# Gate products of 20 more tiles made on chip in a decoder block with retrieved experts

## The chip, the core and the metric

The kernel runs on one core of one Trainium2 chip. The core has five engines with instruction streams of their own: TensorE (PE, matmuls), VectorE (DVE, elementwise work), ScalarE (ACT, activation functions and copies), GpSimd (POOL, here mostly gathers of table rows) and SyncE (SP, which issues transfers). They meet at semaphores. The metric is the time of one execution in device microseconds (us), median of several runs; lower is better.

## What is computed

One decoder block in fp32 over 512 tokens of 1024 channels. Three gated token mixers come first (forgetting attention, sliding-window attention, attention over a memory), and their merged output is added to the input. The change concerns what follows, a retrieval of experts:

```
def peer_ffn(h, w_q, keys1, keys2, u, v):
    q = (h @ w_q).reshape(B, S, PEER_HEADS, 2, half)
    ...
    sv, si = lax.top_k(cand, PEER_TOPK)
    experts = e1 * N_KEYS + e2
    gates = jax.nn.softmax(sv, axis=-1)
    ...
        a = jnp.einsum('cd,ced->ce', h_c, u[e_c])
        act = jax.nn.gelu(a, approximate=False) * g_c
        return jnp.einsum('ce,ced->cd', act, v[e_c])
```

Every token picks 8 x 16 = 128 of 16384 experts. For each of them it takes the dot product with a row of u, a gelu, the gate, and adds that multiple of a row of v.

## The kernel before

The 512 tokens are four blocks of 128. For blocks 0 and 1 the picked rows of u and v are gathered one by one by POOL (L833) and used by DVE: the dot product with a row of u is L843, the addition of a row of v is L852. A call of `step` uses one such row and has the next ones fetched, up to six ahead in the stage of the change (`AHEAD + MORE`), four ahead later.

Blocks 2 and 3 (256 tokens) are done densely over all experts, in 128 tiles of 128 experts. A tile k is one slice of u: eight matmuls of 128 x 128 by 256 tokens (`dense_u`, L971), then a gelu on ACT (L973) into `ga(k)`, a slot of 128 experts x 256 tokens. Slots 0 to 51 lie in the tile `soon`, later ones in `late`. In the end each slot is multiplied by the gates of its experts, zero for an expert that a token hasn't picked, and goes through the matmuls with v (`dense_v`).

The gates become dense in the spread stage, one loop over 64 groups of four tokens (run three ahead for the first part):

- `build_sides`: DVE compares a row of numbers with the picked expert's two indices, which gives two one-hot tiles `o` (L1026); ACT multiplies one by the gates (L1029).
- a call of `step` in four of five rounds (`STEPS_N` = 0.8).
- `spread`: PE multiplies the two one-hot tiles for each of the four tokens (L1041), which leaves in a bank of PSUM 128 gates of 128 tiles for each token. For the first `KEPT` = 32 tiles, whose activations are ready, DVE multiplies the gates straight into the slots (L1044, 32 tiles x 4 tokens). ACT copies the gates of the other 96 tiles to three stage tiles (L1047), and every eighth group SP writes these to memory (`gd`, L1051).
- four steps of the generator `dense_u`: one step to begin a tile, eight with a matmul each, one with the gelu. Ten steps make a tile, so 25 tiles (32 to 56) are computed beside 64 groups.

Behind it lies the v stage, a loop over the 128 tiles: for tile k the slot and the rows of v are split into high and low parts (L1089 and L1091 on ACT, L128 and L1094 on DVE), and PE makes 24 matmuls (L142 to L144). From tile 32 on, SP first reads the gates of four tiles at a time back (`gq`, L1065, two transfers each) and DVE multiplies (L1086). Tiles 57 to 127 of u run in this loop as well, every second one with split operands (L958, L960), and so do the remaining gathered rows.

PE, DVE and POOL run in the order in which the program is written from here on (`manual_schedule`); ACT and SP are ordered by the scheduler.

Of the kernel before, what the change touches and what calls it, by code (L numbers as in the profile page):

```python
# [7 lines left out]
F32 = mybir.dt.float32  # L8
# [4 lines left out]
AF = mybir.ActivationFunctionType  # L13
# [14 lines left out]
ND = len(DENSE)  # L28
TD = 128 * ND
FIRST_U, COVER, DURING, AFTER = 8, 24, 25, 0  # L30
KEPT = FIRST_U + COVER
SPILT = (128 - KEPT) // 3
AMONG, UNWEIGHED = 1.0, 14
LAG = FIRST_U + COVER + DURING + AFTER
GA_LATE = 6
# [10 lines left out]
GT = 4  # L46
TG = 32
GK = 4
WSLOT = 4 * 264
# [7 lines left out]
def tile_block(ctx: ExitStack, tc: tile.TileContext, t: dict, out: bass.AP):  # L57
    nc = tc.nc
    V, A, PE, G = nc.vector, nc.scalar, nc.tensor, nc.gpsimd
# [6 lines left out]
    wp = ctx.enter_context(tc.tile_pool(name="wp", bufs=3))  # L66
# [4 lines left out]
    def bank(tag):  # L71
        return psum.tile([128, 512], F32, tag=tag, name=tag, bufs=BANKS[tag])
# [26 lines left out]
    def load_raw(src, n):  # L99
        loads[0] += 1  # L100
        pool = early[0] if early and loads[0] % (RAW_MORE + 3) >= 3 else wp
        raw = pool.tile([128, WSLOT], F32, tag="raw", name="raw")
        fill(raw, src, n)
        return raw
# [35 lines left out]
    def mm3(ps, l, r, first=True, last=True):  # L140
        (lh, ll), (rh, rl) = l, r
        PE.matmul(ps, lh, rh, start=first, stop=False)  # L142
        PE.matmul(ps, lh, rl, start=False, stop=False)  # L143
        PE.matmul(ps, ll, rh, start=False, stop=last)  # L144
# [775 lines left out]
    soon = dp.tile([128, LAG + 1 - GA_LATE, TD], F32, name="ga", bufs=1)  # L920

    def ga(k):
        s = k % (LAG + 1)
        return soon[:, s] if s <= LAG - GA_LATE else late[0][:, s - (LAG + 1 - GA_LATE)]
# [11 lines left out]
        else:  # L936
            nc.sync.dma_start(u_raw[k], t["uT"][k])

    u_ring, u_next = [None, None], [FIRST_U]

    def fetch_u_to(k):
        while u_next[0] <= min(k, NK - 1):
            fetch_u(u_next[0])
            u_next[0] += 1

    def split_u(k):
        return k >= LAG and (k - LAG) % U_SPLIT > 0

    def dense_u(k):

        if k < FIRST_U:
            w = load_raw(t["uT"][k], D)[:, :D]
        else:
            fetch_u_to(min(k + URING - 1, LAG + 1) if k < LAG else k)
            w = u_raw.pop(k)
        if split_u(k):
            hi, lo = (gp[0].tile([128, D], F32R, tag=tag, name=tag, bufs=1) for tag in ("uhi", "ulo"))
            A.copy(hi, w)  # L958
            yield
            V.tensor_sub(lo, w, hi.bitcast(F32))  # L960
            yield
            ps, hi, lo = bank("mm"), *(x.rearrange("p (n w) -> p n w", n=KC) for x in (hi, lo))
            for dc in range(KC):
                mm3(ps[:, :TD], (hi[:, dc], lo[:, dc]), [x[dc] for x in h2s], dc == 0, dc == KC - 1)
            A.activation(ga(k), ps[:, :TD], AF.Gelu)
            return
        w = w.rearrange("p (n w) -> p n w", n=KC)
        yield
        ps = bank("mm")
        for dc in range(KC):  # L970
            PE.matmul(ps[:, :TD], w[:, dc], h2f[dc], start=dc == 0, stop=dc == KC - 1)  # L971
            yield
        A.activation(ga(k), ps[:, :TD], AF.Gelu)  # L973

    f = Found(found, BIG)
    h2T = [chunks(x) for x in pair(BIG)]
# [2 lines left out]
    with tc.tile_pool(name="qb", bufs=2) as qq:  # L979
        turn([x1[b] for b in GROUPS[1]], g2, *h2T)  # L980
        spent, dg, credit[0] = 0.0, None, 0.0
        for cost in search(qq, h2T, f, BIG):
            spent += cost
            if dg is None and spent > 12.0:
                V.tensor_copy(rstd[:, 1:NB], factors(sums, BIG))
                dg = diagonals(rstd[:, 2:NB], ND)
                turn([x1[b] for b in DENSE], g2, h2f, None, dg)
            credit[0] += cost
            while credit[0] >= PER_ROW and NJ <= done[0] < known[0]:
                credit[0] -= PER_ROW  # L990
                with tc.high_priority(-LATER):
                    step(apart=True)
            if k_u < FIRST_U and spent > 104.0 / FIRST_U * (k_u + 1):
                list(dense_u(k_u))
                k_u += 1
# [4 lines left out]
    gd = [dram.tile([128, NK // GK, 128 // TG, GK * TG], F32, name=f"gd{i}") for i in range(ND)]  # L1000


    slots, sides, stage = {}, {}, {}
# [4 lines left out]
    def turn_block(i):  # L1008

        ps = bank("acc")  # L1010
        b = DENSE[i]
        for k, src in enumerate((*chosen[b], gate[b])):
            PE.transpose(ps[:, k * 128:(k + 1) * 128], src, ident)
        eT = sp.tile([128, 3, 128], F32, tag="eT", name="eT", bufs=2)
        A.copy(eT.rearrange("p a b -> p (a b)"), ps[:, :384])
        slots[i] = eT

    def tokens(n):
        i, q = divmod(n, 128 // GT)
        return i, q * GT, slice(q * GT, (q + 1) * GT)  # L1020
# [11 lines left out]
    def spread(n):  # L1032
        i, t0, _ = tokens(n)
        o = sides.pop(n)
        if t0 % TG == 0:

            stage[0] = [wp.tile([128, WSLOT], F32, tag=tag, name="st")[:, :SPILT * TG].rearrange(
                "p (k t) -> p k t", t=TG) for tag in (("whi", "wlo") * 3)[n // (TG // GT) % 2 * 3:][:3]]
        ps = bank(("sc", "tp")[n % 2]).rearrange("p (t k) -> p t k", t=4)
        for u in range(GT):  # L1040
            PE.matmul(ps[:, u], o[:, 1, u], o[:, 0, u], start=True, stop=True)  # L1041
        c = t0 % TG
        kept = soon[:, :KEPT, i * 128 + t0:i * 128 + t0 + GT]
        V.tensor_mul(kept, ps[:, :, :KEPT].rearrange("p t k -> p k t"), kept)  # L1044
        for hf in range(3):
            k0 = KEPT + hf * SPILT
            A.copy(stage[0][hf][:, :, c:c + GT], ps[:, :, k0:k0 + SPILT].rearrange("p t k -> p k t"))  # L1047
        if c + GT == TG:
            for hf in range(3):
                k0 = KEPT + hf * SPILT  # L1050
                nc.sync.dma_start(gd[i][:, k0 // GK:(k0 + SPILT) // GK, t0 // TG],  # L1051
                                  stage[0][hf].rearrange("p (a k) t -> p a (k t)", k=GK))

    def get_gates(k, part):

        k -= k % GK
        if not KEPT <= k < NK or not 0 <= part < GQ_PARTS:
            return
# [52 lines left out]
    while k_u < FIRST_U + COVER:  # L1111
        if k_u == FIRST_U + UNWEIGHED:
            list(weigh(cp, f, 1))
        list(dense_u(k_u))
        k_u += 1
# [12 lines left out]
    spreading = ExitStack()  # L1128
    sp = spreading.enter_context(tc.tile_pool(name="sp", bufs=1))
    tile_u = None  # L1130
    turn_block(0)
    for n in range(AHD):
        build_sides(n)
    credit[0] = 0.0
    for n in range(AHD, NBAT + AHD):
        if n < NBAT:
            build_sides(n)
        if n == NBAT - PLAIN_ROWS:
            ahead[0] = AHEAD
        if n == NBAT - V_EARLY:  # L1140
            for k in range(VFAR):
                fetch_v(k)
        credit[0] += STEPS_N
        while credit[0] >= 1.0 and done[0] < known[0]:
            credit[0] -= 1.0
            step()
        if (n + 4) % PER == 0 and n + 4 < NBAT:
            turn_block((n + 4) // PER)
        spread(n - AHD)
        for _ in range(STEPS_U):  # L1150
            if tile_u is None and FIRST_U + COVER + n * DURING // NBAT >= k_u:
                tile_u = dense_u(k_u)
                next(tile_u)
                k_u += 1
            elif tile_u is not None and next(tile_u, 1):
                tile_u = None
    for _ in tile_u or ():
        pass
    share[0] = 0.0
    spreading.close()  # L1160
    gp = [ctx.enter_context(tc.tile_pool(name="gp", bufs=2))]
# [127 lines left out]
```

## Time and profile before

| | us |
|---|---|
| median of 3 runs (lowest, highest) | 1620.98 (1619.58, 1623.15) |
| profiled execution | 1613.45 |
| its span, first to last instruction | 1611.6 |
| spread stage, first one-hot tile to last gate product | 857.4 to 1004.1 |
| v stage, first matmul | 1006.5 |

The profile is of one execution; times in it are us from the span's start. The profiled execution is 7.5 us under the median of the runs. In a row of the timeline stand the start, the length, the engine, the line, the operation, the tile written and those read, and in brackets the idle time ahead of it with what ended it. A group's row has the busy time, the mean in ns and the idle time.

### The profile page before, as it was taken

The numbers are of one execution on the slowest core, as the hardware profiler recorded it, in microseconds if no ns is written. First come the engines' busy times: TensorE is split into PE (matmuls) and PEld (weight loads), VectorE is DVE, ScalarE is ACT, GpSimd is POOL, SyncE is SP. The second block draws the span as 40 slices with busy tenths as digits, with TensorE's granted clock in tenths as the row PEclk, the third lists the DMA queues.
The fourth block names the chain that finished last, engine by engine and source line by source line (L and its number), as shares of the span: only waits on it lengthen the run. The fifth ranks groups of instructions, "written<-read, shape, count | busy, mean of one in ns | idle before, by whom it ended". The sixth has DMA issues, their size and how long they took to land.

```text
span 1611.6 us, 26380 instructions
## 1 busy us (share of the span) xinstructions
PE 1532.9 (95%) x9030; PEld 1377.0 (85%) x9030; DVE 1406.2 (87%) x2721; ACT 782.9 (49%) x1782; POOL 780.6 (48%) x625
## 2 busy tenths in 40 slices
PE   5999999998998999998999999899999999999998
PEld 5999899988887989987888999688888888888887
DVE  5677458889888999999999999889899999999997
ACT  6787437645445443553116888344344343433432
POOL 1100011767566455588664333556655566555551
PEclk9999999999998999999999999999999999999999
DMA  8586753899998899967898999999999999999995
GB/s 300 176 283 223 236 196 118 285 358 310 326 344 287 280 360 342 326 203 264 320 404 304 367 385 350 379 394 394 399 409 407 395 411 408 410 412 409 406 407 215
DMA packets 180406, 531.85 MB, mean 330 GB/s; under 512 B 17456, under 2 KB 46384, under 8 KB 180272
## 3 DMA queue, kind: packets, MB, share of 16 engines
q0 software_dynamic: 73728, 268.47, 44.6%
q1 hardware_dynamic: 96752, 226.04, 38.6%
q10 hardware_dynamic: 9792, 35.66, 5.6%
q8 instruction: 71, 1.16, 0.3%
q14 instruction: 63, 0.52, 0.1%
HBM read 515.42 MB, written 14.68 MB: 329 GB/s over the span
## 4 chain that ended last, share of the span: by engine, by line
PE 36%; DVE 22%; DMA 17%; issue 15%; POOL 7%; ACT 2%; SPq 0%; DVEq 0%; POOLq 0%; ACTq 0%
DMA row<-in_peer_u_dram,eidx 8%; DMA row<-in_peer_v_dram,eidx 7%; POOL row L833 6%; PE mm L143 6%; PE mm L144 6%; PE mm L142 6%; DVE mg L852 6%; DVE o L1026 3%; DVE scr L843 3%; PE mm L971 3%; DVE wlo L128 2%; PE mm L295 2%; PE sc L142 1%; PE sc L143 1%; PE sc L144 1%
## 5 line engine op out<-in xcount | busy, mean ns | idle before, releaser
L833 POOL DMA_INDIRECT row<-in_peer_v_dram,eidx x256 | 346.0, 1351 | 269.2 <-DVE mg L852 150.0
L833 POOL DMA_INDIRECT row<-in_peer_u_dram,eidx x256 | 330.9, 1292 | 271.6 <-DVE scr L843 161.8
L843 DVE SCALAR_TENSOR_TENSOR scr<-row,own 128x1024 bf16<-128x1024 f32 x256 | 314.5, 1228 | 31.7 <-DMA row<-in_peer_u_dram,eidx 29.6
L128 DVE TENSOR_TENSOR wlo<-raw,whi 128x1024 fp32r<-128x1024 f32 (+1 forms) x243 | 305.6, 1259 | 36.3 <-ACT whi L116 35.7
L852 DVE SCALAR_TENSOR_TENSOR mg<-row,acts,mg 128x1024 f32<-128x1024 f32 x237 | 304.4, 1285 | 20.5 <-DMA row<-in_peer_v_dram,eidx 18.2
L971 PE MATMUL mm<-h2f,hhi 128*128 128x256 f32 x976 | 223.2, 379 | 1.6 <-ACT ga L973 1.6
L971 PEld LDWEIGHTS mm<-h2f,hhi 128*128 128x128 f32 x976 | 182.5, 190 | 26.6 <-ACT ga L973 2.0
L116 ACT CAST whi<-raw 128x1024 fp32r<-128x1024 f32 (+1 forms) x148 | 155.0, 1050 | 90.2 <-PE mm L143 47.1
L189 POOL TENSOR_TENSOR rsy<-rsv,mhalf 128x4 f32<-128x4 f32 (+5 forms) x25 | 38.8, 1553 | 219.8 <-DVE rsv L188 126.3
L1089 ACT CAST ah<-ga 128x256 fp32r<-128x256 f32 x116 | 47.0, 407 | 150.8 <-PE tp L143 118.1
L1091 ACT CAST whi<-raw 128x1024 fp32r<-128x1024 f32 x96 | 100.4, 1046 | 39.6 <-PE tp L144 26.0
L142 PE MATMUL mm<-hhi,whi 128*128 128x384 f32 x320 | 110.8, 347 | 5.9 <-ACT ga L973 4.6
L143 PE MATMUL mm<-hlo,whi 128*128 128x384 f32 x320 | 111.2, 347 | 0.0
L144 PE MATMUL mm<-hhi,wlo 128*128 128x384 f32 x320 | 110.1, 344 | 0.0
L142 PE MATMUL mm<-whi,hhi 128*128 128x256 f32 (+1 forms) x360 | 104.6, 292 | 3.0 <-DVE g L572 1.9
L142 PE MATMUL sc<-whi,ah 128*128 128x512 f32 x256 | 107.3, 419 | 0.0
L143 PE MATMUL sc<-wlo,ah 128*128 128x512 f32 x256 | 101.1, 395 | 3.4 <-DVE wlo L128 3.4
L143 PE MATMUL mm<-wlo,hhi 128*128 128x256 f32 (+1 forms) x360 | 103.1, 287 | 0.2 <-DVE wlo L128 0.2
L144 PE MATMUL mm<-whi,hlo 128*128 128x256 f32 (+1 forms) x360 | 101.7, 284 | 0.0
L973 ACT ACTIVATE ga<-mm 128x256 f32<-128x256 f32 x84 | 31.7, 379 | 143.5 <-PE mm L971 143.4
L144 PE MATMUL sc<-whi,al 128*128 128x512 f32 x256 | 101.1, 395 | 0.0
L142 PE MATMUL tp<-whi,ah 128*128 128x512 f32 x256 | 100.6, 393 | 0.0
(289 smaller groups left out, 3941.8 us busy)
## 6 DMA issues: line engine op xcount, KB each, us to landing
raw<-in_peer_v_dram SPq DMA_DIRECT2D x96, 512.0 KB, 8.1
hhi<-in_uT_dram ACTq DMA_DIRECT2D x68, 512.0 KB, 7.7
raw<-in_w_tr_dram SPq DMA_DIRECT2D x48, 512.0 KB, 5.0
raw<-in_w_nat_dram SPq DMA_DIRECT2D x40, 512.0 KB, 5.7
last<-in_peer_v_dram SPq DMA_DIRECT2D x32, 512.0 KB, 7.4
hhi<-in_uT_dram SPq DMA_DIRECT2D x28, 512.0 KB, 6.7
raw<-in_w_o_dram SPq DMA_DIRECT2D x24, 512.0 KB, 6.1
hlo<-in_uT_dram SPq DMA_DIRECT2D x24, 512.0 KB, 7.2
```

Source lines behind the costliest of these rows:

```text
L116: A.copy(hi[:, :n * w], raw[:, :n * w])
L128: V.tensor_sub(lo, raw, hi.bitcast(F32))
L142: PE.matmul(ps, lh, rh, start=first, stop=False)
L143: PE.matmul(ps, lh, rl, start=False, stop=False)
L144: PE.matmul(ps, ll, rh, start=False, stop=last)
L833: G.indirect_dma_start(out=r, out_offset=None, in_=t["peer_" + tab], in_offset=bass.IndirectOffsetOnAxis(ap=eidx[b][:, j:j + 1], axis=0))
L843: V.scalar_tensor_tensor(scr, r, 1.0, h2n[b], op0=OP.mult, op1=OP.mult, accum_out=acts[b][:, c]))
L852: V.scalar_tensor_tensor(x1[b], r, acts[b][:, c], x1[b], op0=OP.mult, op1=OP.add))
L971: PE.matmul(ps[:, :TD], w[:, dc], h2f[dc], start=dc == 0, stop=dc == KC - 1)
L1026: V.tensor_tensor(o, numbers[:, None, None, :].to_broadcast([128, 2, GT, NK]), eT[:, :2, ts, None].to_broadcast([128, 2, GT, NK]), op=OP.i ...
L1089: A.copy(ah, a)
L1091: A.copy(hi, raw)
```

## The change

20 more tiles, 32 to 51, have their gates multiplied on chip. Their activations aren't there yet when the spread stage begins, so POOL first writes 1.0 into their slots, and the product of each group (now 52 tiles x 4 tokens) leaves the gate itself there. When such a tile's matmuls are done, the gelu is written back into its PSUM bank, and a product on DVE puts it into the slot (`weigh_kept`): this is called after the third matmul of the tile that follows, so one round of the loop later.

A slot is complete only after all 64 groups and its own product, in either order: tile 32's product comes after the first groups, and the later groups then multiply their gates into finished activations, which gives the same as in the other order.

76 tiles remain for the stage tiles and for memory, in pieces of 28, 24 and 24, and the v stage reads and multiplies from tile 52 on.

```diff
-KEPT = FIRST_U + COVER
-SPILT = (128 - KEPT) // 3
+KEPT = 52
+SPILT = (28, 24, 24)
...
             PE.matmul(ps[:, :TD], w[:, dc], h2f[dc], start=dc == 0, stop=dc == KC - 1)
+            if dc == 2:
+                weigh_kept()
             yield
-        A.activation(ga(k), ps[:, :TD], AF.Gelu)
+        if FIRST_U + COVER <= k < KEPT:
+            A.activation(ps[:, :TD], ps[:, :TD], AF.Gelu)
+            unkept.append((k, ps))
+        else:
+            A.activation(ga(k), ps[:, :TD], AF.Gelu)
+
+    def weigh_kept():
+        while unkept:
+            n, ps = unkept.pop()
+            V.tensor_mul(ga(n), ps[:, :TD], ga(n))
...
-        for hf in range(3):
-            k0 = KEPT + hf * SPILT
-            A.copy(stage[0][hf][:, :, c:c + GT], ps[:, :, k0:k0 + SPILT].rearrange("p t k -> p k t"))
-        if c + GT == TG:
-            for hf in range(3):
-                k0 = KEPT + hf * SPILT
-                nc.sync.dma_start(gd[i][:, k0 // GK:(k0 + SPILT) // GK, t0 // TG],
-                                  stage[0][hf].rearrange("p (a k) t -> p a (k t)", k=GK))
+        k0 = KEPT
+        for nk, st in zip(SPILT, stage[0]):
+            A.copy(st[:, :, c:c + GT], ps[:, :, k0:k0 + nk].rearrange("p t k -> p k t"))
+            if c + GT == TG:
+                nc.sync.dma_start(gd[i][:, k0 // GK:(k0 + nk) // GK, t0 // TG],
+                                  st.rearrange("p (a k) t -> p a (k t)", k=GK))
+            k0 += nk
...
+    G.memset(soon[:, FIRST_U + COVER:KEPT], 1.0)
     turn_block(0)
     for n in range(AHD):
         build_sides(n)
...
     for _ in tile_u or ():
         pass
+    weigh_kept()
```

On DVE, four rounds into the spread stage, the order was this (`mg` is the sum to which a gathered row of v is added, `ga` are the slots, `o` the one-hot tiles; in brackets the semaphores waited for):

```order
L852 SCALAR_TENSOR_TENSOR mg_2246<-row,acts_177,mg_2246 128x1024 [waits DMASW1_49,DVE_49]
L1044 TENSOR_TENSOR ga<-tp,ga 128x32x4 [waits PE_49]
L1026 TENSOR_TENSOR o<-tg,eT 128x1024 [waits Activation_49]
L852 SCALAR_TENSOR_TENSOR mg_2246<-row,acts_177,mg_2246 128x1024 [waits DMASW2_49,DVE_49]
L1044 TENSOR_TENSOR ga<-sc,ga 128x32x4 [waits PE_49]
```

In the changed kernel the same place on DVE, with its own line numbers (L1055 is the former L1044, L1037 the former L1026, L984 is in `weigh_kept`):

```order
L852 SCALAR_TENSOR_TENSOR mg_2246<-row,acts_177,mg_2246 128x1024 [waits DMASW1_49,DVE_49]
L1055 TENSOR_TENSOR ga<-tp,ga 128x52x4 [waits PE_49]
L984 TENSOR_TENSOR ga<-mm,ga 128x256 [waits DVE_49,Activation_49]
L1037 TENSOR_TENSOR o<-tg,eT 128x1024
L852 SCALAR_TENSOR_TENSOR mg_2246<-row,acts_177,mg_2246 128x1024 [waits DMASW2_49]
L1055 TENSOR_TENSOR ga<-sc,ga 128x52x4 [waits DVE_49,PE_49]
```

The gate product is wider, and right behind one of them stands the product of a finished tile, which waits for DVE's own earlier write and for ACT's gelu; 20 such products lie in the stage.

On POOL, at the beginning of the spread stage, the gathers of rows stood like this:

```order
L833 DMA row_9416<-in_peer_v_dram,eidx0_176 128x1024 [waits DMASW3_49,DVE_49]
L833 DMA row_9422<-in_peer_v_dram,eidx0_176 128x1024 [waits DMASW4_49,DVE_49]
L833 DMA row_9425<-in_peer_v_dram,eidx0_176 128x1024
L833 DMA row_9490<-in_peer_v_dram,eidx0_176 128x1024 [waits DMASW5_49,DVE_49]
L833 DMA row_9512<-in_peer_v_dram,eidx0_176 128x1024 [waits DMASW7_49,DMASW6_49,DVE_49]
```

In the changed kernel POOL has there:

```order
L833 DMA row_9416<-in_peer_v_dram,eidx0_176 128x1024 [waits DMASW3_49,DVE_49]
L833 DMA row_9422<-in_peer_v_dram,eidx0_176 128x1024 [waits DMASW4_49,DVE_49]
L833 DMA row_9425<-in_peer_v_dram,eidx0_176 128x1024
L1141 MEMSET ga_7513 128x5120
L833 DMA row_9491<-in_peer_v_dram,eidx0_176 128x1024 [waits DMASW5_49,DVE_49]
```

The memset waits for nothing and stands ahead of the first gather that belongs to the spread stage.

More of the change, by code (lines that the diff above doesn't have):

```diff
@@ L937, in fetch_u @@
             nc.sync.dma_start(u_raw[k], t["uT"][k])
-    u_ring, u_next = [None, None], [FIRST_U]
+    u_ring, u_next, unkept = [None, None], [FIRST_U], []
     def fetch_u_to(k):
@@ L1035, in spread @@
         if t0 % TG == 0:
-            stage[0] = [wp.tile([128, WSLOT], F32, tag=tag, name="st")[:, :SPILT * TG].rearrange(
-                "p (k t) -> p k t", t=TG) for tag in (("whi", "wlo") * 3)[n // (TG // GT) % 2 * 3:][:3]]
+            stage[0] = [wp.tile([128, WSLOT], F32, tag=tag, name="st")[:, :nk * TG].rearrange(
+                "p (k t) -> p k t", t=TG) for nk, tag in zip(SPILT, (("whi", "wlo") * 3)[n // (TG // GT) % 2 * 3:])]
         ps = bank(("sc", "tp")[n % 2]).rearrange("p (t k) -> p t k", t=4)
```

## The prediction

> **What bounds the kernel now.** I read the page's busy shares first, then busy time by stage, then the waits of each stage, then the order in time on VectorE (DVE) and TensorE (PE). The page's shares are of a span of 1611.6 us:
>
> ```profile
> PE 1532.9 (95%) x9030; PEld 1377.0 (85%) x9030; DVE 1406.2 (87%) x2721; ACT 782.9 (49%) x1782; POOL 780.6 (48%) x625
> ```
>
> An average says nothing of one stage. The view of stretches has the spread stage (857 to 1004 us: gates are spread, tiles 32 to 56 computed) and pieces of the v stage behind it. Columns: stretch and length, busy time of PE, PE weight loads, DVE, ACT and POOL, granted PE clock, DMA share, GB/s.
>
> ```profile
> 857.00:1004.00 147.00, 144.87 (x919) 134.50 (x920) 145.33 (x206) 123.35 (x483) 49.86 (x50) 1.00 0.98 349
> 1026.00:1032.00 6.00, 5.42 (x24) 5.32 (x25) 5.93 (x10) 0.60 (x2) 3.15 (x3) 0.50 0.99 366
> ```
>
> ```profile
> 1100.00:1200.00 100.00, 98.72 (x506) 85.06 (x505) 88.89 (x138) 40.12 (x62) 58.02 (x40) 1.00 1.02 404
> 1200.00:1300.00 100.00, 98.08 (x499) 83.64 (x499) 90.83 (x134) 39.30 (x61) 57.14 (x39) 1.00 1.02 403
> ```
>
> In the spread stage PE and DVE are both full, with 144.87 and 145.33 of 147 us. In the v stage PE has 98 of 100, DVE 89 to 91. A busy PE can hide waits, so here are its starts in the spread stage (start, length, line; every fp32 matmul leaves two records, so x8 is four matmuls):
>
> ```profile
> 918.78 1.05 PE L1041 MATMUL sc<-o 128*128 128x128 f32 x8
> 919.67 1.89 PE L971 MATMUL mm<-h2f,hlo 128*128 128x256 f32 x8
> 921.40 1.05 PE L1041 MATMUL tp<-o 128*128 128x128 f32 x8
> ```
>
> From start to start four spread matmuls take 0.89 us and four dense ones 1.73 us. The stage has 64 groups of the first and 25 tiles of two groups of the second: 64 x 0.89 + 50 x 1.73 = 143.5 us. So PE does work all that time. DVE in the same place:
>
> ```profile
> 916.50 1.31 DVE L852 SCALAR_TENSOR_TENSOR mg<-row,acts,mg 128x1024 f32<-128x1024 f32 x1
> 917.69 0.32 DVE L1044 TENSOR_TENSOR ga<-sc,ga 128x128 f32<-128x128 f32 x1
> 917.89 1.25 DVE L1026 TENSOR_TENSOR o<-tg,eT 128x1024 f32<-128x1024 f32 x1
> 919.02 0.31 DVE L1044 TENSOR_TENSOR ga<-tp,ga 128x128 f32<-128x128 f32 x1
> ```
>
> One instruction follows the other with no hole; a start comes before the end of the last, so what an instruction costs is its distance to the next start. The waits of this stage (857 to 1006 us; sum, times, longest):
>
> ```profile
> PE sc L1041 <- issue: 2.6, 1, 2.6
> DVE ga L1044 <- PE sc L1041: 1.2, 1, 1.2
> DVE ga L1044 <- PE tp L1041: 0.5, 2, 0.3
> ```
>
> DVE waited 1.7 us in all, late in the stage. The two engines come out level: work added to DVE here has 1.7 us of room and no more.
>
> **The change, part by part.** *Wider gate products.* Each of the 64 products L1044 goes from 32 x 4 = 128 elements a partition to 52 x 4 = 208. By the rows above 128 elements take 0.20 us (917.69 to 917.89) and 1024 take 1.13 us (917.89 to 919.02), so 0.93 / 896 = 1.04 ns an element: 80 more are 0.083 us, and 64 of them 5.3 us, all on the full DVE.
>
> *Twenty moved products.* Tiles 32 to 51 leave the v stage's product L1086 and get one in the spread stage, of the same 256 elements:
>
> ```profile
> 1208.27 0.42 DVE L1086 TENSOR_TENSOR ga<-gq,ga 128x256 f32<-128x256 f32 x1
> 1208.61 1.22 DVE L843 SCALAR_TENSOR_TENSOR scr<-row,own 128x1024 bf16<-128x1024 f32 x1
> ```
>
> That is 0.34 us each, 6.8 us added to the spread stage and 6.8 us taken from the v stage. The moved ones read PSUM, where L1086 reads SBUF. L1044 reads PSUM too, and its 0.20 us less 128 x 1.04 ns leaves 0.07 us; L1086's 0.34 us less 256 x 1.04 ns leaves 0.07 us as well, so I charge nothing for PSUM. [...]
>
> *Their place.* Each moved product stands right behind a wide product that writes the same slots, and waits for DVE itself. What that costs shows in a chain of 128-element instructions earlier, where L786 needs L785's result and L852 needs nothing of L786:
>
> ```profile
> 831.45 0.29 DVE L785 TENSOR_TENSOR rj<-rj,p 128x128 f32<-128x128 f32 x1
> 831.77 0.29 DVE L786 TENSOR_TENSOR rj<-p,rj 128x128 f32<-128x128 f32 x1
> 831.98 1.28 DVE L852 SCALAR_TENSOR_TENSOR mg<-row,acts,mg 128x1024 f32<-128x1024 f32 x1
> ```
>
> 0.32 us against 0.21: 0.11 to 0.12 us a time, 20 times 2.4 us; the lower bound is nothing. The gelu that it also waits for stands on ACT ahead of copies that are an iteration older, and ACT has 24 us free, so I charge no wait for it.
>
> Together DVE gets 5.3 + 6.8 + 2.4 = 14.5 us more in a stage with 1.7 us of room: **+12.8 us**. PE has the same matmuls; it runs at most two or three groups ahead and then waits for the one-hot tiles. The next tile but one now waits for DVE to leave the bank, where it waited for ACT; that only bounds PE's lead. Queued behind DVE are the copies to the stage tiles and their DMAs, which come as much later.
>
> *The memset.* It stands on POOL between these two gathers, and the first wide product waits for it:
>
> ```profile
> 854.74 1.02 POOL L833 DMA_INDIRECT row<-in_peer_v_dram,eidx  x1 [0.30 <-issue]
> 856.41 1.86 POOL L833 DMA_INDIRECT row<-in_peer_v_dram,eidx  x1 [0.65 <-DVE mg L852]
> ```
>
> ```profile
> 861.91 0.28 DVE L1044 TENSOR_TENSOR ga<-sc,ga 128x128 f32<-128x128 f32 x1
> ```
>
> It can start at 855.8 us and has 6.1 us until 861.9. No row has a large memset on POOL. The nearest is POOL's own two-input add:
>
> ```profile
> L849 POOL TENSOR_TENSOR mg<-mg,row 128x1024 f32<-128x1024 f32 x19 | 45.5, 2396 | 0.4
> ```
>
> 2.34 ns an element makes 12.0 us of 5120 elements, so 5.9 us late; DVE's 1.1 ns makes 5.6 us and hides. A memset reads nothing, so I take a value near the short end: **+0.5 us**, with 0 and +5.9 as ends. The gather behind it comes some us later; its row is one of up to six in flight (AHEAD + MORE), and 0.8 x 64 = 51 rows are used in 147 us, one in 2.9 us, which covers that.
>
> *Less to copy and carry.* ACT's copies and the gate writes shrink by 20 of 96 tiles, and 10 of 48 gate reads go: 20 x 128 x 256 x 4 B = 2.6 MB each way. ACT is not full and nothing of PE or DVE waits for gate reads, so by itself: 0.
>
> *Between the stages.* From the last L1044 on, DVE has no hole but one, a row's DMA, and PE waits for DVE there:
>
> ```profile
> 1003.86 0.29 DVE L1044 TENSOR_TENSOR ga<-tp,ga 128x128 f32<-128x128 f32 x1 [0.33 <-PE tp L1041]
> ...
> 1022.68 1.23 DVE L843 SCALAR_TENSOR_TENSOR scr<-row,own 128x1024 bf16<-128x1024 f32 x1 [2.24 <-DMA row<-in_peer_u_dram,eidx]
> ```
>
> ```profile
> 1026.58 0.58 PE L144 MATMUL mm<-hlo,ulo 128*128 128x256 f32 x1 [4.39 <-DVE ulo L960]
> ```
>
> So a late DVE makes all later work late. With less gate traffic the row may land earlier, between 0 and 2.2 us; I take **-1.0**. After PE's 4.39 us of waiting the stretch 1026 to 1032 has a granted clock of 0.50, which cost some 3.0 us. If the wait shrinks enough that goes too; I leave it in. [...]
>
> *The v stage.* The products of tile 32, the first, and of tile 52, the first in the small late tile, are the starts of these two groups:
>
> ```profile
> L1086 DVE TENSOR_TENSOR ga<-gq,ga x84: 414/420/426, 1150.2 to 1600.0; 128x256 f32<-128x256 f32 x84
> ...
> L1086 DVE TENSOR_TENSOR late<-gq,late x12: 416/418/423, 1244.8 to 1545.0; 128x256 f32<-128x256 f32 x12
> ```
>
> So tiles 32 to 51 have their products between 1150 and 1245 us. PE's waits there, and DVE's for rows, in the windows 1140 to 1195 and 1195 to 1250:
>
> ```profile
> DVE scr L843 <- DMA row<-in_peer_u_dram,eidx: 2.5, 3, 1.5
> PE mm L144 <- DVE ulo L960: 1.3, 1, 1.3
> ```
>
> ```profile
> DVE scr L843 <- DMA row<-in_peer_u_dram,eidx: 2.6, 3, 1.4
> ```
>
> The second window has no wait of PE above. So 6.8 us less on DVE can give back PE's 1.3 us: **-1.3**; with two waits just behind, in the window 1255 to 1285, at most -3.2:
>
> ```profile
> PE mm L144 <- DVE ulo L960: 1.3, 1, 1.3
> PE sc L143 <- DVE wlo L128: 0.6, 1, 0.6
> ```
>
> Sum: 12.8 + 0.5 - 1.0 - 1.3 = **+11.0 us**. The profiled execution took 1613.45 us and would take 1624.5; the timed median stands 7.5 us above it, at 1620.98, and I carry the difference over: 1632.0 us.
>
> **Rivals.** *The give-back case (faster).* DVE, with its row DMAs, sets PE's pace in the v stage, so its relief counts in full: 6.8 us of products, the 5.1 us of row waits between 1140 and 1250, and between the stages the 4.4 us and the half clock's 3.0: 19.3 against 13.3 spent, so 1615.0 us. It decides from 13.3 us given back. For it: DMA share 1.02. Against: PE's 98 busy of 100 and its one wait of 1.3 us. Chance 0.04.
>
> *All ends low (no change).* No wait behind the wide products (-2.4), the row's DMA and the half clock gone (-5.2), three waits of PE gone (-3.2): 12.8 - 10.8 = +2.0, 1623.0 us. What a measurement here can tell from no change is about 0.2%, 3.2 us. Each is possible, all together hardly: 0.06.
>
> *A slow memset (slower still).* POOL writes at its add's pace, the first wide product waits 5.9 us, and both engines stand: +16.4, 1637.4 us. For it: the only large row of POOL. Against: that one reads two inputs. Chance 0.10.
>
> My forecast has 0.80. Its own ends come from the parts above; with the rivals on both sides I take 1623.5 to 1637.5 us, which leaves out most of the first two rivals and values still above. Faster 0.04, same 0.06, slower 0.90.
>
> **What would show it.** Right: the last wide product ends 12 to 14 us later, counted from the first one-hot tile; DVE still without holes; PE's busy time unchanged there, with new waits for one-hot tiles (through ACT's scaling) that sum to some 12 us; the wide product 0.28 to 0.30 us from start to start, the moved one 0.34 with some 0.12 of waiting ahead; the v stage shorter by 1 to 3 us. Wrong: a spread stage longer by under 8 us, which would say that DVE had room I did not see; a v stage shorter by over 5 us, which would say that DVE or DMA paced PE; a hole on DVE ahead of the first wide product, which gives the memset's length.

## The result and the profile after

| | before | after |
|---|---|---|
| median, us (lowest to highest of 6 runs) | 1620.95 (1617.50 to 1623.22) | 1634.96 (1627.75 to 1642.04) |
| ratio to before (95% interval) | | 1.0087 (1.0063 to 1.0110) |
| profiled execution (span) | 1613.45 (1611.6) | 1642.04 (1640.3) |
| spread stage: first one-hot tile to the start of the last wide product | 857.4 to 1003.9: 146.5 | 864.3 to 1031.2: 166.9 |
| from there to the end | 607.7 | 609.1 |

The change costs 14.0 us, against 11.0 forecast: slower, and inside the range. The two profiled executions lie at opposite ends of their kernels' runs, the one of after 7.1 us above its median, so their spans, 28.7 us apart, aren't to be compared as they stand. 6.9 us of that lie ahead of the spread stage, where nothing was changed. In this execution DVE waited 5.5 us there for a copy on ACT; the profiles of two kernels below that have the spread stage of before show such a wait too (4.0 and 4.5 us, first one-hot tile at 862.0 and 863.1 us), and that of before shows none. Inside the stage the profile has 20.4 us more, behind it 1.4 more.

The busy shares of after, and the view of stretches (columns as before): the spread stage over the same 147 us, its end, and the piece of the v stage in which the 20 moved products were.

```profile
PE 1543.2 (94%) x9030; PEld 1383.6 (84%) x9030; DVE 1413.8 (86%) x2721; ACT 782.4 (48%) x1782; POOL 777.0 (47%) x626
```

```profile
857.00:1004.00 147.00, 134.87 (x830) 123.03 (x829) 139.04 (x192) 104.27 (x408) 45.59 (x43) 1.00 0.90 308
1020.00:1040.00 20.00, 15.82 (x69) 13.41 (x70) 13.67 (x28) 12.67 (x47) 5.01 (x5) 0.83 0.76 225
1150.00:1245.00 95.00, 95.00 (x489) 81.84 (x489) 83.94 (x125) 38.02 (x59) 56.25 (x40) 1.00 1.00 391
```

PE, DVE and ACT ran as many instructions as before, POOL one more, the memset. PE did 830 matmul records in the 147 us instead of 919. Near the stage's end, from 1020 us on, PE and DVE were both below full, and the clock averaged 0.83. In the v stage PE was busy in all of the 95 us, where before it was in 93.66:

```profile
1150.00:1245.00 95.00, 93.66 (x481) 80.38 (x480) 87.56 (x142) 37.40 (x58) 54.23 (x38) 1.00 1.02 407
```

DVE's order in time in the middle of the stage:

```profile
875.41 1.27 DVE L852 SCALAR_TENSOR_TENSOR mg<-row,acts,mg 128x1024 f32<-128x1024 f32 x1
876.61 0.37 DVE L1055 TENSOR_TENSOR ga<-tp,ga 128x208 f32<-128x208 f32 x1
877.08 0.42 DVE L984 TENSOR_TENSOR ga<-mm,ga 128x256 f32<-128x256 f32 x1
877.42 1.21 DVE L1037 TENSOR_TENSOR o<-tg,eT 128x1024 f32<-128x1024 f32 x1
```

A wide product alone takes 0.28 to 0.29 us to the next start, a moved one 0.34 (877.08 to 877.42). With a moved one behind it, the wide product takes 0.47: the wait of the moved product, which needs the write just ahead, is 0.18 to 0.19 us, not 0.12. So DVE's new work is 64 x 0.085 = 5.4 us, 20 x 0.34 = 6.8 and 20 x 0.185 = 3.7: 15.9 us. Less the 1.7 us of room, that explains 14.2 of the 20.4. The rest stands in the waits of this stage (845 to 1032 us; sum, times, longest):

```profile
PE mm L971 <- DVE ga L984: 9.8, 9, 1.4
...
PE tp L1052 <- ACT o L1040: 3.8, 1, 3.8
...
DVE ga L1055 <- PE tp L1052: 3.1, 2, 2.9
...
DVE ga L1055 <- PE sc L1052: 2.9, 1, 2.9
...
PE sc L1052 <- ACT o L1040: 1.1, 1, 1.1
...
DVE ga L984 <- ACT o L1040: 0.5, 1, 0.5
```

PE's nine waits for L984 are the sign that DVE is the slower engine: a moved product holds the PSUM bank, and PE's next tile but one waits for it. They cost nothing by themselves. DVE's own waits do: 6.5 us inside the stage, and all but 0.5 of them are at the very end. The chain to them begins on ACT (last figure of a row: idle time and what ended it):

```profile
1015.07 1.04 ACT L1101 CAST whi<-raw 128x1024 fp32r<-128x1024 f32 x1 [2.40 <-issue]
1016.02 1.27 ACT L1040 ACTIVATE o<-o,eT 128x128 f32<-128x128 f32 x4
...
1019.08 1.04 ACT L1101 CAST whi<-raw 128x1024 fp32r<-128x1024 f32 x1 [1.39 <-issue]
...
1020.31 2.23 ACT L137 CAST hlo<-h2f 128x256 fp32r<-128x256 f32 x7
1022.44 1.28 ACT L1040 ACTIVATE o<-o,eT 128x128 f32<-128x128 f32 x4
```

The casts of the v stage's first two tiles (L1101) and seven of eight casts of h (L137), all work of the next stage, stand on ACT ahead of scalings (L1040) of the last one-hot tiles: the scalings of four tiles come after the first cast and of three after the second. The first cast had to wait 2.40 us, the second 1.39, and the scalings waited behind them. The casts' own time counts as well: between the end of the copies ahead of the second cast (1017.7) and the scaling at 1022.44 lie 4.7 us, of which 1.4 are waiting and 3.3 are casts and a gelu. Before, two tiles and then one stood behind these casts, and the casts had nothing to wait for; here are both, the second with the last scaling:

```profile
994.26 1.03 ACT L1091 CAST whi<-raw 128x1024 fp32r<-128x1024 f32 x1
...
1000.02 1.07 ACT L1091 CAST whi<-raw 128x1024 fp32r<-128x1024 f32 x1
1000.97 1.30 ACT L1029 ACTIVATE o<-o,eT 128x128 f32<-128x128 f32 x4
```

PE, then DVE, at the same place after the change:

```profile
1022.89 2.07 PE L1052 MATMUL tp<-o 128*128 128x128 f32 x8 [3.76 <-ACT o L1040]
1024.76 3.62 PE L971 MATMUL mm<-h2f,hhi 128*128 128x256 f32 x8
```

```profile
1025.01 0.37 DVE L1055 TENSOR_TENSOR ga<-tp,ga 128x208 f32<-128x208 f32 x1 [2.85 <-PE tp L1052]
...
1029.41 0.37 DVE L1055 TENSOR_TENSOR ga<-sc,ga 128x208 f32<-128x208 f32 x1 [2.89 <-PE sc L1052]
```

PE waits 3.76 us for a scaled tile, and its next four dense matmuls take 3.62 us (1.89 before, at full clock; from 1022.9 to 1028.2 us the granted clock was 0.50); DVE waits for PE once for the delay and once more for the slow clock behind it.

The memset has its length now, on POOL:

```profile
857.05 4.38 POOL L1141 MEMSET ga<- 128x5120 f32 x1
861.60 0.94 POOL L833 DMA_INDIRECT row<-in_peer_v_dram,eidx  x1 [0.17 <-issue]
```

4.38 us for 5120 elements a partition, 0.86 ns each; it ended at 861.4, and the first wide product came at 868.79 us for other reasons.

### The profile page after: what moved, and what is told of

It reads as the page before. It is cut to its first block, busy times and chain, and to the rows that moved or that the text cites. A ratio compares the mean times of both kernels' runs of the same rounds, so it can differ in the third digit from the quotient of the medians.

```text
span 1640.3 us, 26415 instructions
## 1 busy us (share of the span) xinstructions
PE 1543.2 (94%) x9030; PEld 1383.6 (84%) x9030; DVE 1413.8 (86%) x2721; ACT 782.4 (48%) x1782; POOL 777.0 (47%) x626
## 4 chain that ended last, share of the span: by engine, by line
PE 38%; issue 19%; DMA 18%; DVE 13%; POOL 10%; ACT 2%; SPq 0%; POOLq 0%; DVEq 0%; ACTq 0%
DMA row<-in_peer_v_dram,eidx 10%; POOL row L833 9%; PE mm L971 8%; DMA row<-in_peer_u_dram,eidx 6%; PE mm L143 5%; PE mm L142 5%; PE mm L144 5%; DVE mg L852 3%; DVE wlo L128 2%; PE mm L295 2%; DVE o L1037 1%; PE sc L142 1%; PE sc L144 1%; PE sc L143 1%; PE tp L144 1%
## 5 line engine op out<-in xcount | busy, mean ns | idle before, releaser
L833 POOL DMA_INDIRECT row<-in_peer_v_dram,eidx x256 | 340.3, 1329 | 287.0 <-DVE mg L852 201.2
L843 DVE SCALAR_TENSOR_TENSOR scr<-row,own 128x1024 bf16<-128x1024 f32 x256 | 312.3, 1220 | 31.9 <-DMA row<-in_peer_u_dram,eidx 26.8
L852 DVE SCALAR_TENSOR_TENSOR mg<-row,acts,mg 128x1024 f32<-128x1024 f32 x237 | 303.5, 1280 | 18.4 <-DMA row<-in_peer_v_dram,eidx 15.3
L1101 ACT CAST whi<-raw 128x1024 fp32r<-128x1024 f32 x96 | 100.4, 1046 | 36.5 <-PE tp L144 15.9
L143 PE MATMUL tp<-wlo,ah 128*128 128x512 f32 x256 | 100.5, 392 | 0.0
```

The source lines that it names most:

```text
L833: G.indirect_dma_start(out=r, out_offset=None, in_=t["peer_" + tab], in_offset=bass.IndirectOffsetOnAxis(ap=eidx[b][:, j:j + 1], axis=0))
L843: V.scalar_tensor_tensor(scr, r, 1.0, h2n[b], op0=OP.mult, op1=OP.mult, accum_out=acts[b][:, c]))
L852: V.scalar_tensor_tensor(x1[b], r, acts[b][:, c], x1[b], op0=OP.mult, op1=OP.add))
L1101: A.copy(hi, raw)
```

## The experiments

The account to be tested, theory A in the expectations: DVE's added work in the spread stage costs its full length; the casts that ACT's order puts ahead of the scalings cost some 6 us more; and the work taken from the v stage gives next to nothing back. Each expectation names its rivals.

**The v stage alone.** The kernel before, with the products and gate reads of tiles 32 to 51 left out of the v stage, and nothing added elsewhere. Those 20 tiles go on without their gates.

```diff
-        if not KEPT <= k < NK or not 0 <= part < GQ_PARTS:
+        if not 52 <= k < NK or not 0 <= part < GQ_PARTS:
...
-        if k >= KEPT:
+        if k >= 52:
```

> The kernel before with the v stage's half of the change alone: no gate reads and no products on DVE for tiles 32 to 51, the spread stage as before (the gates of these 20 tiles are left out of the result). Theory A, PE sets the pace of the v stage: of the 6.8 us taken from DVE there only PE's short waits come back, so 1 to 3 us less than before. Rival B, DVE with its row transfers sets the pace there: 7 to 12 us less than before.

Measured: 1618.44 us, ratio 1.0002 (0.9986 to 1.0019). 20 products and ten gate reads fewer make no difference that can be measured; the gain of 1 to 3 us that was expected didn't show, and up to 2.3 us of it lie within the interval. The same piece of the v stage as above, in this kernel:

```profile
1150.00:1245.00 95.00, 95.00 (x490) 81.88 (x489) 83.34 (x125) 38.59 (x60) 56.22 (x40) 1.00 1.01 394
```

PE's hole of 1.3 us is closed, as forecast, and DVE has 4.2 us less to do; but PE was already at 93.66 of 95, and more than that can't come back. So the change has hardly more than a cost side.

**The casts held behind the scalings.** The changed kernel, with the scalings and the casts of the next stage (of the first v tiles and of h) kept on ACT in the order in which they are written.

```diff
-            A.activation(o[:, 0, u], o[:, 0, u], AF.Copy, scale=eT[:, 2, ts.start + u:ts.start + u + 1])
+            tc.keep_in_program_order(A.activation(
+                o[:, 0, u], o[:, 0, u], AF.Copy, scale=eT[:, 2, ts.start + u:ts.start + u + 1]))
...
+        if n == NBAT:
+            cast[0] = wp.tile([128, WSLOT], F32R, tag="whi", name="whi")[:, :D]
+            tc.keep_in_program_order(A.copy(cast[0], v_raw[0]))
...
-        split(h2s[0][dc], h2s[1][dc], h2f[dc])
+        tc.keep_in_program_order(A.copy(h2s[0][dc], h2f[dc]))
+        V.tensor_sub(h2s[1][dc], h2f[dc], h2s[0][dc].bitcast(F32))
```

> The changed kernel, with ACT's cast of the first rows of v and the casts for the split operands held behind the last scaling of a one-hot tile. Theory A, these casts stalled ACT and through it PE and DVE at the end of the spread stage (6.0 us of DVE waiting for PE in the profile of the changed kernel): 5 to 8 us less than the changed kernel, so 6 to 9 us over the kernel before, and DVE waits under 1 us there. Rival C, DVE's added work alone sets the end of the stage and the stall is only where its room shows: within 2 us of the changed kernel.

Measured: 1626.51 us, ratio 1.0052 (1.0031 to 1.0073), 8.5 us below the changed kernel by the medians, 5.7 by the two ratios, each of which is against the kernel before beside it. The two intervals overlap a little; the profiles show the difference more sharply. The waits of its spread stage:

```profile
PE mm L971 <- DVE ga L984: 8.4, 8, 1.4
...
DVE ga L984 <- ACT o L1040: 0.5, 1, 0.5
```

No wait of DVE for PE is left, and the stage takes 160.7 us: 14.2 more than before, which is the 15.9 of DVE work less the 1.7 of room. The waits at the end came from the casts.

The whole costs 8.4 us by the ratio and not 14.2, because behind the stage this kernel needs 601.7 us, 6.0 less than the kernel before with its 607.7. From the start of the last wide product to the ninth v tile (its subtraction into `al` on DVE) it takes 36.6 us where the kernel before takes 40.4: 3.8 of the 6.0 us are won there, where PE waited less and kept its full clock (rows below, under "Between the stages"). The other 2.2 us are not taken apart.

**The same hold on the kernel before.** If the hold were a gain by itself, the experiment above would not say what the change's casts cost. The edit is the same, with the kernel before under it.

> The kernel before with the same hold on ACT's casts as in the run with casts held, as its control. Theory A, before had no stall to lose: within 3 us of the kernel before. Rival F, the hold is a gain in any kernel, and the change lost nothing by its casts: 6 to 9 us less than before, as much as it gained on the changed kernel.

Measured: 1621.17 us, ratio 1.0002 (0.9985 to 1.0018), stage 146.5 us. The hold gains nothing where the casts don't wait.

**The change again.** The changed kernel without an edit, to see whether the stall at the stage's end belonged to one execution.

> The changed kernel as it is, once more, beside the others on one chip. Theory A: 1631 to 1638 us; in its profile 15 to 16 us more work on DVE between the first one-hot tile and the last wide product than before, and 5 to 7 us of waiting for PE at the end of that stage, behind casts on ACT that wait for transfers. Rival H, the stall at the end was a matter of that one execution: DVE waits under 2 us there.

Measured: 1633.67 us, ratio 1.0095 (1.0062 to 1.0129), stage 167.0 us. ACT and PE at the stage's end:

```profile
1011.12 1.05 ACT L1101 CAST whi<-raw 128x1024 fp32r<-128x1024 f32 x1 [2.66 <-DMA gd<-st]
```

```profile
1018.49 2.08 PE L1052 MATMUL tp<-o 128*128 128x128 f32 x8 [3.30 <-ACT o L1040]
1020.36 3.62 PE L971 MATMUL mm<-h2f,hhi 128*128 128x256 f32 x8
```

The stall is the same in its place, its length and the slow clock behind it. Here the releaser of the first cast is named, a transfer of gates to memory (`gd`), and it is named again with the product apart (next run):

```profile
1012.27 1.05 ACT L1099 CAST whi<-raw 128x1024 fp32r<-128x1024 f32 x1 [2.49 <-DMA gd<-st]
```

The kernel says why a cast waits for it. The stage tiles of `spread` and the results of these casts are both allocated under the tag `whi`, so a cast can write only when the gates that lay in its buffer have left for memory. The last such transfers ahead of the first cast on SP's queue, in the kernel before and in the changed kernel's first profile:

```profile
988.25 2.37 SPq L1051 DMA_DIRECT2D gd<-st  x3
```

```profile
1010.56 3.63 SPq L1060 DMA_DIRECT2D gd<-st  x3
```

Before, ACT started the first cast 6.0 us after 988.25, and three tiles were scaled in between. In the changed kernel it stood ready 2.1 us after 1010.56, with one tile scaled in between, and started 4.5 us after it. So ACT's order alone would make this wait; a late transfer isn't needed for it. For the second cast no releaser is named, and why the scheduler chose this order is not shown.

**The moved products apart from the wide ones.** `weigh_kept` is called right behind `build_sides`, so that the moved product stands at another place among DVE's rows.

```diff
-            if dc == 2:
-                weigh_kept()
...
             build_sides(n)
+        weigh_kept()
```

> The changed kernel with the moved product not right behind the wide product but behind the one-hot tile that follows it, so that in four of five rounds a gathered row stands between it and the next wide product. Theory A, 0.18 us of waiting on each of 20 products (3.7 us in the profile of the changed kernel) is part of the cost: 2 to 4 us less than the changed kernel. Rival E, that wait is taken back elsewhere, since the end of the stage is set by ACT's casts: within 1.5 us of the changed kernel.

Measured: 1630.60 us, ratio 1.0066 (1.0042 to 1.0091), 3.1 under the changed kernel that ran beside it (the change again), whose interval overlaps. Two places on DVE:

```profile
931.30 0.41 DVE L982 TENSOR_TENSOR ga<-mm,ga 128x256 f32<-128x256 f32 x1
931.82 0.38 DVE L1053 TENSOR_TENSOR ga<-tp,ga 128x208 f32<-128x208 f32 x1
...
938.46 0.42 DVE L982 TENSOR_TENSOR ga<-mm,ga 128x256 f32<-128x256 f32 x1
938.79 1.28 DVE L852 SCALAR_TENSOR_TENSOR mg<-row,acts,mg 128x1024 f32<-128x1024 f32 x1
```

With a row's instruction behind it the moved product takes 0.33 us; where a wide product follows at once it takes 0.52. So the wait of 0.19 us belongs to two dependent products in a row. The stage is 160.9 us; DVE's waits for PE also fell, to 2.3 us, so the gain isn't the dependent wait's alone, and its size is not sharply measured.

**The moved products on POOL.** On top of the held casts, the gelu goes to SBUF, and POOL multiplies.

```diff
-            A.activation(ps[:, :TD], ps[:, :TD], AF.Gelu)
-            unkept.append((k, ps))
+            act = sp.tile([128, TD], F32, tag="act", name="act", bufs=2)
+            A.activation(act, ps[:, :TD], AF.Gelu)
+            unkept.append((k, act))
...
-            V.tensor_mul(ga(n), ps[:, :TD], ga(n))
+            G.tensor_tensor(ga(n), act, ga(n), op=OP.mult)
```

> The run with casts held, and the 20 moved products made by POOL from a gelu that ACT writes to SBUF. DVE keeps only the wider gate products. Theory A, DVE's load makes the stage: 10.5 us less work than with casts held, so a stage of 149 to 153 us against 160.7, and 1616 to 1621 us where the kernel before has 1620. Rival G, POOL's products hold up DVE's wide products, or slow DVE while both work, by as much: the stage stays over 157 us.

Measured: 1619.56 us, ratio 0.9996 (0.9982 to 1.0010), stage 150.0 us. The group of products on POOL, and DVE beside it:

```profile
L985 POOL TENSOR_TENSOR ga<-act,ga 128x256 f32<-128x256 f32 x20 | 14.6, 730 | 43.2 <-ACT o L1041 24.5 <-DVE ga L1057 11.5 <-ACT act L977 7.2
```

```profile
931.73 0.74 POOL L985 TENSOR_TENSOR ga<-act,ga 128x256 f32<-128x256 f32 x1 [2.16 <-ACT o L1041]
```

```profile
931.22 0.36 DVE L1057 TENSOR_TENSOR ga<-tp,ga 128x208 f32<-128x208 f32 x1
931.50 1.21 DVE L1038 TENSOR_TENSOR o<-tg,eT 128x1024 f32<-128x1024 f32 x1
932.63 1.27 DVE L852 SCALAR_TENSOR_TENSOR mg<-row,acts,mg 128x1024 f32<-128x1024 f32 x1
933.83 0.36 DVE L1057 TENSOR_TENSOR ga<-sc,ga 128x208 f32<-128x208 f32 x1
934.11 1.21 DVE L1038 TENSOR_TENSOR o<-tg,eT 128x1024 f32<-128x1024 f32 x1
```

POOL needs 0.73 us a product, twice DVE's time, and it costs nothing, because POOL had some 100 us free in the stage (45.59 of 147 busy in after) and DVE's rows beside it keep their pace: the one-hot tile beside the product above takes 1.13 us to the next start (931.50 to 932.63), and over the stage the wide products took 354 to 368 ns and the one-hot tiles 1203 to 1224, in after 360 to 375 and 1209 to 1225. What is left of the change is the wider product: 5.4 less 1.7 is 3.7 us, and the stage is 3.5 longer. The kernel equals the one before; it doesn't beat it.

**Room made by moving rows.** If DVE lacks room in the spread stage, fewer gathered rows there make some: `STEPS_N` from 0.8 to 0.6 takes 13 rows out, which then run in the v stage. Once on the changed kernel, once on the kernel before as a control.

```diff
-SPARE, STEPS_N = 4, 0.8
+SPARE, STEPS_N = 4, 0.6
```

> The changed kernel with 0.6 instead of 0.8 gathered rows a round in the spread stage: 38 rows there instead of 51, the other 13 are used in the v stage. Theory A, the loss is DVE time in the spread stage: 13 rows of 1.2 us are 15.6 us less DVE work there, which makes that stage 147 to 153 us from first one-hot tile to last product, and the rows fit into DVE's free tenth of the v stage: 1617 to 1626 us on the scale of the kernel before at 1621. Rival C, the loss comes from the order on ACT alone and not from DVE's load: the stage stays over 160 us and the time over 1630 us.

> The kernel before with 0.6 instead of 0.8 rows a round, as a control for the run with rows moved. Theory A, PE needs 143.5 us for the spread stage whatever DVE does, and DVE gains room it cannot use: within 3 us of the kernel before, or slower by up to 6 us for the 13 rows in the v stage. Rival D, the kernel before was itself short of DVE in the spread stage: 3 to 8 us less than before.

Measured on the change: 1631.87 us, ratio 1.0070 (1.0051 to 1.0090); on the kernel before: 1633.57 us, ratio 1.0096 (1.0074 to 1.0117). Both expectations missed. The spread stage did what was expected: 148.0 us on the change, 148.2 on the kernel before, in which DVE now had the room and waited for PE:

```profile
DVE ga L1044 <- PE sc L1041: 8.9, 13, 2.3
DVE ga L1044 <- PE tp L1041: 7.2, 14, 0.9
```

The two measured against each other are the change on a kernel whose DVE has room: stage and time are the same within the noise (148.0 and 148.2, 1631.87 and 1633.57 us), so there the change costs nothing.

But the time behind the stage grew to 622.6 and 623.3 us, by 13.5 and 15.6 us, about 1.0 to 1.2 us a row. The waits between 1040 and 1580 us, of the kernel before and of the one with the rows moved:

```profile
DVE scr L843 <- DMA row<-in_peer_u_dram,eidx: 11.1, 14, 2.0
PE mm L144 <- DVE ulo L960: 10.0, 12, 1.5
```

```profile
DVE scr L843 <- DMA row<-in_peer_u_dram,eidx: 22.7, 28, 2.3
PE mm L144 <- DVE ulo L960: 21.5, 14, 2.4
```

And a stretch of the v stage with the rows moved:

```profile
1300.00:1400.00 100.00, 95.85 (x482) 82.16 (x482) 93.05 (x107) 38.78 (x59) 58.24 (x40) 0.98 1.02 402
```

The transfers already fill their engines (DMA share 1.02 at 402 GB/s; before 1.03 at 410 in the same stretch), so a row more is a transfer more: 128 x 1024 x 4 B = 0.52 MB at 0.40 MB a us is an estimated 1.3 us. DVE waits for the rows, and PE for DVE. So the v stage seems to have two limits at once, PE's and the transfers', and takes no row for nothing. A rival is open: POOL waited in this window for DVE to give a row's buffer back, 83.8 us behind L843 and 107.4 behind L852 (86.3 and 98.5 with the rows moved), so the limit may be the four rows in flight and not the transfer engines; no run changed their number.

## Why the prediction was right, and where it wasn't

| term, us | forecast | measured |
|---|---|---|
| wide products | +5.3 | 64 x 0.085 = 5.4 |
| moved products | +6.8 | 20 x 0.34 = 6.8 |
| wait behind a wide product | +2.4 | 20 x 0.185 = 3.7 |
| DVE's room | -1.7 | -1.7 (stage of held casts: +14.2) |
| DVE's waits in the stage, 6.0 of them at its end | 0 | +6.5 |
| memset | +0.5 | 0 |
| row and half clock between the stages | -1.0 | about -0.4; half clock still there |
| v stage | -1.3 | nothing measurable |
| whole | +11.0 | +14.0 (median); +21.8 from the stage on in the profile |

**Which engine pays.** Right: DVE and PE were level, and DVE's new work counted in full. Held casts showed it (+14.2 us with no stall), and the products on POOL showed it from the other side (-10.7 us of stage for work that took twice as long elsewhere). With rows moved away the change cost nothing.

**The sum** came near in part by luck. With casts held the change costs 8.4 us, 2.6 less than the forecast, because the time behind the spread stage shrank by 6.0 us where I took 2.3; the stall, which I had at nothing, adds 5.7 by the ratios and brings it to 14.

**The wait behind the wide product** was mis-sized: 0.18 to 0.19 us in place of 0.12. I took it from 128-element instructions; behind products of 208 and 256 elements it is longer. That their size makes it so isn't shown.

**The step that failed** is "ACT is not full and nothing of PE or DVE waits for gate reads, so by itself: 0". For the gelu alone, "ACT has 24 us free, so I charge no wait for it" held: DVE's products waited 0.5 us in all. But free time on ACT said nothing of its order at the stage's end. There the scheduler put the casts of the next stage ahead of more scalings than before, and sooner behind the gate transfers that their buffers wait for. It cost 6.0 us of DVE waits in the profile, and 5.7 to 8.5 us in the time, the held casts against the changed kernel. "DVE still without holes" and "12 to 14 us later" were wrong for that reason.

**PE's new waits** were forecast for the one-hot tiles. Most came for the PSUM bank of the moved product (9.8 us, nine times): the bank that "only bounds PE's lead" was the shorter lead of the two. That changed nothing in the time.

**PSUM.** I charged nothing for the source in PSUM. The moved product takes 424 to 426 ns (its group of 20), the v stage's, from SBUF, 414 to 426, and both 0.34 us from start to start. So these rows show no charge for it.

**The memset** was hidden, so the slow rival (12.0 us) fell. POOL's writing, 0.86 ns an element, is nearer to DVE's pace, 1.04, than to its own two-input add, 2.34.

**Between the stages** the row's DMA came a little earlier: DVE's wait for it was 1.8 us (2.2 before) and PE's 3.96 (4.39), so the half clock stayed, as I had it (0.50 from 1053.6 to 1059.0 us). With the casts held the wait was 3.31 us and the half clock was gone:

```profile
1053.66 0.58 PE L144 MATMUL mm<-hlo,ulo 128*128 128x256 f32 x1 [3.96 <-DVE ulo L960]
1054.03 0.41 PE L142 MATMUL mm<-hlo,uhi 128*128 128x256 f32 x1
```

```profile
1037.30 0.39 PE L144 MATMUL mm<-hlo,ulo 128*128 128x256 f32 x1 [3.31 <-DVE ulo L960]
1037.53 0.28 PE L142 MATMUL mm<-hlo,uhi 128*128 128x256 f32 x1
```

The matmuls behind the wait take 0.41 us in the first, which is the changed kernel, and 0.28 in the second. In the change again a wait of 3.50 us at this place was followed by matmuls of 0.41 us as well, with the product apart one of 2.49 by matmuls of 0.28. Behind the wait of 3.30 us at the stage's end of the change again four dense matmuls took 3.62 us, as long as in the changed kernel's first profile at a granted clock of 0.50, while behind the wait of 3.31 us the matmuls took the full pace of 0.28, so near this length the waiting alone doesn't tell.

**The v stage** gave PE its 1.3 us in that piece, but no run made that show in the time, and behind the stage the changed kernel took 609.1 us against 607.7 where 1 to 3 us less were forecast. The give-back rival (1615.0) is refuted by the v stage alone.

**What stays open.** From the stage on, both profiles of the changed kernel show 21.8 us more than before, their ratios 14.1 and 15.4; for held casts, the product apart and POOL the same sum (+8.2, +9.9 and +0.7 us) is within 1.3 us of the ratio (+8.4, +10.7 and -0.6). Perhaps the stall, which hangs on when transfers land, is shorter in most executions: the changed kernel's runs spread over 14.3 us, those of before over 5.7 (11.9 and 9.9 in the later comparisons). No run shows it. Nor was it tried which of the held casts, those of v or those of h, does the most.

## What to carry to other kernels

Price moved work by the room in the stage it goes to and by the limits of the stage it leaves: here the one had 1.7 us of room and in the other PE was busy for 93.66 of 95 us, so it could only lose, except on an engine with real room, even at half the speed. And where a scheduler orders an engine, don't charge its part at nothing because it is half idle: look at the stage's end for work of the next stage, the more so if it can wait for a transfer, ahead of work that others wait for, and pin it.

## What the hardware showed unexpectedly

- On DVE the second of a wide and a moved product, which needs the write just ahead, started 0.18 to 0.19 us later than otherwise (0.47 against 0.285 us with the wide one first, 0.52 against 0.33 with the moved one first); with a row's instruction between them the wait was gone (0.33).
- The casts in the way on ACT were paid several times: ACT idle 2.40 and 1.39 us, PE 3.76, then four matmuls at 3.62 in place of 1.89 us, then DVE 2.85 and 2.89.
- A memset of 128x5120 fp32 on POOL took 4.38 us, a two-input product of 128x256 there 0.73 us, and a one-hot tile on DVE beside it 1.13 us to the next start, as in the kernel before.
- 13 gathered rows more in the v stage cost 13.5 to 15.6 us, at a DMA share of 1.02.
